# Sixteen experts taken in turns of their groups, with the first results gathered while the last weights are split

## The chip, the cores and the metric

The kernel runs on one core of a Trainium2 chip. Its time is the device time of that core in microseconds (us), the median of several executions; lower is better. The engines that matter here are PE (TensorE, matmuls), DVE (VectorE), ACT (ScalarE) and POOL (GpSimd), which also issues the indirect DMAs (gathers by a list of row numbers), and SP (SyncE), which issues all the other DMAs. Each engine works through its own queue in order.

## The reference

One layer of a decoder trunk over 1024 tokens (and 16 meta tokens) of width 1024: four token mixers, a norm, and then a hierarchical mixture of experts, which alone the change touches. A token picks the best of 4 groups and then the best two of the 4 experts in that group; its output is the weighted sum of the two experts' results, added to the scaled residual stream and normed.

```python
g_sel = jnp.argmax(g_logit, -1)
p_grp = jnp.take_along_axis(jax.nn.softmax(g_logit, -1), g_sel[:, None], 1)
e_logit = jnp.take_along_axis(e_logit, g_sel[:, None, None], 1)[:, 0]     # the 4 experts of that group
top_val, top_idx = lax.top_k(e_logit, TOP_K_INNER)                         # TOP_K_INNER = 2
w = jax.nn.softmax(top_val, -1) * p_grp
e_idx = g_sel[:, None] * EXPERTS_PER_GROUP + top_idx
...
for e in range(N_EXPERTS):                                                 # N_EXPERTS = 16, N_GROUPS = 4
    hid = jax.nn.silu(xf @ w_gate[e]) * (xf @ w_up[e])
    y = y + gate[:, e:e + 1] * (hid @ w_down[e])
...
h = _layer_norm(DN_ALPHA * h + moe_out, ln2_g[l], ln2_b[l])
```

## The kernel before

The mixers and their projections take most of the time; the change does not touch them. Then `Routing.norm` and `Routing.route` norm and route the tokens in 8 tiles of 128. `route` finds the group and the two experts with `max` and `max_index` on DVE and writes them as two one-hot tiles `A[0]` and `A[1]` of 128x16 (tokens by experts); from running counts of these it gives each token a row in the list of each of its two experts. An expert's list holds `CAP` = 192 rows; what goes beyond that is done in a loop after the main part, which runs as often as a count `nov` in memory says, with the expert's number read from `ovx`.

`Experts` runs the 16 experts one after the other. For each one POOL gathers 192 token rows (`xg`, two gathers of 96), PE transposes them (`xT`), and the three weights of the expert come in as six pieces of 128x1024 (512 KB each) on SP's queue. Each piece (`raw`) is split into a rounded part by ACT (`s4h`, `mT0h`, ...) and a rest (`s4l`, ...) by a subtraction, on DVE or POOL: `Pieces.low` asks the planner which of the two would be done sooner. The order of the products is gate of expert e, down of e-1, up of e. `hidden` makes the activations in between: `sg` and `su` are the gate's and up's sums, `th` their product, and `hdh`, `hdl` its two parts, which the down product `py` multiplies. The down result goes through ACT (`ey`) to a DRAM tensor `ys` of 192 rows per expert.

`rest` (written once, in the middle of the expert stage) turns places into `slot`: for each token the rows in `ys` of its two results, the smaller row first, and the weights `wt` in the same order. `ahead` gathers the first result of each of the 8 token tiles from `ys` (`y`, 8 gathers of 512 KB, six buffers, `AHEAD` = 6) and adds it to the residual `h` on DVE. It is started at the place where the last store but one has been written into the program, and reads `ys` up to the 15th expert. `finish` then gathers the second results (`z` and `y`, 8 gathers), which need the last expert's store, adds them, takes mean and variance, norms, and stores the output tile by tile. It uses a square root on ACT, for which `ahead` loads the table with a small activation `t` beforehand.

Everything on PE, DVE, ACT and POOL is put in order by a planner (`Order`): it estimates each engine's time as the program is written, and `Order.run` takes the next step of whichever stream is due at the planner's time of PE. On the chip each engine follows that order, whatever the true times are. The streams of the expert stage, in order of rank, are `hidden`, `tokens`, `rest` and `ahead`; `main`, with PE's products, fills what is left:

```python
o.run([(0, None, x.hidden(W2)), (1, None, x.tokens(W2, ps, scale)), (2, lambda: x.gathered > 2, r.rest(W3, ps, k.ovx, k.ovo, k.nov)),
       (3, lambda: x.stored == NE - 1, ahead(k, x.ys, r))], x.main(W2, ps, free))
```

In the profile nearly all work of the planner has one line, L268 (the helper that records it); tiles tell it apart. `finish` is at L2889 to L2928, its gathers at L2848.

Of the kernel before, what the change touches and what calls it, by code (L numbers as in the profile page):

```python
# [13 lines left out]
OP = mybir.AluOpType  # L14
# [2058 lines left out]
NE = 16  # L2073
CAP = 192
# [96 lines left out]
class Project:  # L2171
# [11 lines left out]
    def more(self):  # L2183

        j = len(self.hs)
        if j < 8:
            self.hs.append(self.pc.add([(self.k.hd[j * 128:j * 128 + 128], lambda r: r)], None))
# [74 lines left out]
class Routing:  # L2262
# [83 lines left out]
    def route(self, j, W, ps):  # L2346

        nc = self.k.nc
        yield from nc.wait(lambda: self.hot == j and j in self.ready)
        lg, mg, me, At = self.lg[:, j], self.mg[:, j], self.me[:, j], self.At[:, j]  # L2350
        A = [a[:, j] for a in self.A]
        ix = W.tile([128, 3, 8], U32, name="mi", bufs=2)
        ng, sel = W.tile([128, 4], F32, name="ng", bufs=2), W.tile([128, 16], F32, name="sel", bufs=2)

        def where(out, i, op):
            n = out.shape[1]
            nc.vector.tensor_tensor(out, self.num[:, 0:n], ix[:, i, 0:1].to_broadcast([128, n]), op=op)

        nc.vector.max(mg, lg[:, 16:24])
        yield  # L2360
        nc.vector.max_index(ix[:, 0], mg, lg[:, 16:24])
        yield
        where(ng, 0, OP.not_equal)
        yield

        nc.vector.scalar_tensor_tensor(sel.rearrange("p (g e) -> p g e", g=4), ng[:, :, None].to_broadcast([128, 4, 4]), -3e38,
# [3 lines left out]
        yield  # L2370
        nc.vector.max_index(ix[:, 1], me[:, 0:8], sel)
        yield
        where(A[0], 1, OP.is_equal)
        yield

        nc.vector.scalar_tensor_tensor(sel, A[0], -3e38, sel, op0=OP.mult, op1=OP.add)
        yield
        nc.vector.max_index(ix[:, 2], me[:, 1:9], sel)
        yield
        where(A[1], 2, OP.is_equal)  # L2380
        yield
        nc.vector.tensor_add(At, A[0], A[1])
        self.hot = j + 1
# [3 lines left out]
        p = ps.tile([128, 512], F32, name="mz", bufs=4)  # L2387
# [5 lines left out]
        s, y = W.tile([128, 2], F32, name="sf"), W.tile([128, 2, 16], F32, name="sy")  # L2393
# [9 lines left out]
        x = self.pix[0:HB, 32 * (j % 2):32 * (j % 2) + 32]  # L2403
# [13 lines left out]
    def rest(self, W, ps, ovx, ovo, nov):  # L2417


        k, nc = self.k, self.k.nc  # L2420
        def t(name, n=1, dt=F32):
            return W.tile([128, 8, n], dt, name=name)
# [17 lines left out]
        p = ps.tile([128, 512], F32, name="py", bufs=4)  # L2440
# [30 lines left out]
        a, b, so, fs = t("oa"), t("ob8"), t("so", 2), t("fs", 2)  # L2471
# [33 lines left out]
        ob, oo, oj = (W.tile([1, 16], F32, name=n) for n in ("ob", "oo", "oj"))  # L2505
# [12 lines left out]
        nc.vector.scalar_tensor_tensor(oj, oo, -float(CAP), oj, op0=OP.mult, op1=OP.add)  # L2518
        nc.vector.scalar_tensor_tensor(oj, ob, float(ROOM), oj, op0=OP.mult, op1=OP.add)
        nc.vector.tensor_scalar(oj, oj, 0.0, float(ROOM * NE - CAP), op0=OP.max, op1=OP.min)  # L2520
        nc.vector.tensor_copy(ovx, ob)
        nc.vector.tensor_copy(ovo, oj)
        nc.vector.tensor_copy(nov, inc[0:1, 15:16])


class Experts:


    def __init__(self, k, I, pieces, h1d, ids, ys, more):
        self.k, self.h1d, self.ids, self.ys, self.pc = k, h1d, ids, ys, pieces  # L2530
        wg, wu, wd = (I["moe_w_" + n][0] for n in ("gate", "up", "down"))
        self.at = {}
        self.order = [("g", 0), ("u", 0)]
        for e in range(1, NE):
            self.order += [("g", e), ("d", e - 1), ("u", e)]
        self.order.append(("d", NE - 1))
        self.used = n = 0
        more()
        for what, e in self.order:
            for m in range(2):  # L2540
                if what == "d":
                    src = (wd[e][m * 128:m * 128 + 128], lambda r: r)
                else:

                    src = ((wg if what == "g" else wu)[e][m * 512:m * 512 + 512].rearrange("(a p) c -> p a c", p=128),
                           lambda r: r.rearrange("p (a c) -> p a c", a=4))
                self.at[what, e, m] = pieces.add([src], lambda n=n: self.place(n), True)
                n += 1
                more()
        self.slots, self.xT, self.acc, self.th, self.hid = [], {}, {}, {}, {}  # L2550
        self.gathered = self.products = self.stored = 0
# [295 lines left out]
def gather(k, ys, ix, y):  # L2847
    k.nc.gpsimd.indirect_dma_start(out=y, out_offset=None, in_=ys, in_offset=bass.IndirectOffsetOnAxis(ap=ix, axis=0))  # L2848


def ahead(k, ys, r):


    nc, pend = k.nc, []

    def add():
        j, y, t = pend.pop(0)
        h = k.h1[j // 4][:, j % 4]
        yield t
        nc.vector.scalar_tensor_tensor(h, y, r.wt[:, j, 0:1], h, op0=OP.mult, op1=OP.add)  # L2860

    for j in range(8):
        if j >= AHEAD:
            yield from add()
        y = k.Y.tile([128, D], F32, name="y", bufs=AHEAD)
        gather(k, ys[0:(NE - 1) * CAP], r.slot[:, j, 0:1], y)
        pend.append((j, y, nc.end))
        yield 0.0
    t = k.Y.tile([128, 1], F32, name="t")
    nc.scalar.activation(t, k.eps, AF.Sqrt)  # L2870
    while pend:
        yield from add()
# [84 lines left out]
def trunk(k, ctx, E, I, pieces, m, x, r):  # L2957
# [45 lines left out]
    W2 = es_x.enter_context(tc.tile_pool(name="xw", bufs=1, **left))  # L3003
    W3 = es_x.enter_context(tc.tile_pool(name="rtr", bufs=1, **left))
    ps = es_x.enter_context(tc.tile_pool(name="xps", bufs=1, space=PSUM))
# [8 lines left out]
    def free():  # L3014
# [3 lines left out]
        for i, n in enumerate(("ln2_g", "ln2_b")):  # L3018
            o.sync.dma_start(k.gb2[:, i], dap(I[n], 0, [[0, 128], [1, D]]))

    o.run([(0, None, x.hidden(W2)), (1, None, x.tokens(W2, ps, scale)), (2, lambda: x.gathered > 2, r.rest(W3, ps, k.ovx, k.ovo, k.nov)),
           (3, lambda: x.stored == NE - 1, ahead(k, x.ys, r))], x.main(W2, ps, free))
    es_x.close()


# [62 lines left out]
```

## Time and profile before

| what | us |
|---|---|
| median of 3 runs (lowest, highest) | 1682.43 (1677.73, 1683.59) |
| the profiled execution | 1686.26 |
| its span | 1684.5 |
| PE busy in the span | 1587.0 (94%) |
| expert products on PE, end of the last `py` | 1631.98 |
| first gather of `finish` begins on POOL | 1640.59 |
| last `fo` product of `finish` begins on PE | 1673.80 |

The profiled execution lies 1.76 us above its span and 3.83 us above the median. The span is read here from its end: the expert stage runs from about 1360 to 1632 us and `finish` from there on; the times in the rows below are counted from the start of the span.

### The profile page before, as it was taken

The page shows a single profiled execution, that of the slowest core. Times are in us where ns is not written, and L with a number is a line of the kernel's source. Part 1 is how long each engine was busy: PE and PEld are TensorE (multiplying, and loading weights), DVE is VectorE, ACT ScalarE, POOL GpSimd, SP SyncE. Part 2 cuts the span into 40 slices and gives each one's busy share as a digit, 9 for nine tenths or more (in the row PEclk, how much of TensorE's full clock was granted, in tenths as well). Part 3 has the DMA queues.
Part 4 walks back from the last instruction along what each step waited for, and adds up shares of the span by engine and source line. Part 5 has one row for each costly group of instructions (what it writes and reads, how often), then busy time and mean ns, then how long its engine had stood idle before and what let it go on. Part 6 is the DMA issues. An engine that isn't in the chain of part 4 may idle for free. (4 is left out here: it accounts for less than half of the span.)

```text
span 1684.5 us, 27808 instructions
## 1 busy us (share of the span) xinstructions
PE 1587.0 (94%) x10020; PEld 1336.2 (79%) x10020; DVE 1114.9 (66%) x2534; ACT 755.7 (45%) x1544; POOL 431.0 (26%) x555
## 2 busy tenths in 40 slices
PE   4999999899999999999999999997999989999985
PEld 3999899788887777777887777775788778898962
DVE  8344755754489898884556477748666668776655
ACT  4334444355544455425444433432121157776645
POOL 5222226831111102123211131126800123111021
PEclk9999999999999999999999998998999989999997
DMA  7874445242322323343211252067512379999855
GB/s 245 240 231 133 146 132 146 80 124 78 91 67 78 83 79 104 95 154 108 69 38 32 86 152 63 28 193 251 180 66 101 126 213 265 287 303 279 269 196 201
DMA packets 240429, 244.86 MB, mean 145 GB/s; under 512 B 39018, under 2 KB 204812, under 8 KB 240288
## 3 DMA queue, kind: packets, MB, share of 16 engines
q1 hardware_dynamic: 234400, 222.08, 43.8%
q0 software_dynamic: 5888, 20.97, 4.4%
q8 instruction: 80, 1.31, 0.3%
q14 instruction: 61, 0.50, 0.1%
HBM read 168.98 MB, written 74.02 MB: 144 GB/s over the span
## 5 line engine op out<-in xcount | busy, mean ns | idle before, releaser
L268 PE MATMUL pj<-hTl,wh 128*128 128x512 f32 (+3 forms) x1184 | 435.5, 368 | 1.0 <-DVE hTl L268 1.0
L268 PE MATMUL pj<-hTh,wh 128*128 128x512 f32 (+3 forms) x1184 | 435.2, 368 | 0.0
L268 PE MATMUL pj<-hTh,wl 128*128 128x512 f32 (+3 forms) x1184 | 431.5, 364 | 0.0
L268 PEld LDWEIGHTS pj<-hTh,wh 128*128 128x128 f32 (+1 forms) x1184 | 225.8, 191 | 26.8 <-issue 2.5
L268 PEld LDWEIGHTS pj<-hTl,wh 128*128 128x128 f32 (+1 forms) x1184 | 225.6, 191 | 26.5 <-issue 1.6
L268 POOL TENSOR_TENSOR wl<-wr,wh 128x256 fp32r<-128x256 f32 (+1 forms) x177 | 137.8, 795 | 422.9 <-ACT wh L268 407.0
L268 PEld LDWEIGHTS pj<-hTh,wl 128*128 128x128 f32 (+1 forms) x1184 | 226.0, 191 | 23.7 <-issue 1.6
L268 ACT COPY pe<-pj 128x384 f32<-128x384 f32 (+3 forms) x84 | 37.4, 445 | 121.9 <-PE pj L268 83.7
L268 DVE SCALAR_TENSOR_TENSOR sc<-rl,wi,sc 128x512 f32<-128x512 f32 (+3 forms) x77 | 58.7, 762 | 42.4 <-ACT rl L268 39.3
L268 ACT CAST wh<-wr 128x256 fp32r<-128x256 f32 (+1 forms) x240 | 85.1, 402 | 1.0 <-DMA wr<-in_w_in_dram 0.9
L268 ACT ACTIVATE pe<-pj 128x512 f32<-128x512 f32 x64 | 38.1, 595 | 100.4 <-PE pj L268 74.8
L268 POOL TENSOR_TENSOR h<-h,g 128x512 f32<-128x512 f32 x46 | 64.7, 1420 | 51.9 <-issue 32.2
L268 POOL DMA_INDIRECT xg<-h1d,ix x32 | 33.7, 1054 | 155.4 <-PE py L268 148.7
L268 ACT ACT_TABLE_LOAD x47 | 60.3, 1283 | 6.3 <-DVE qk L268 2.6
L268 PE MATMUL pg<-xT,mT0h 128*128 128x384 f32 x208 | 62.4, 362 | 0.0
L268 POOL TENSOR_TENSOR sc<-sc,band 128x256 f32<-128x256 f32 (+1 forms) x32 | 24.4, 764 | 124.1 <-DVE sc L268 84.8
L268 PE MATMUL pg<-xT,mT0l 128*128 128x192 f32 x208 | 53.8, 259 | 0.0
L268 DVE TENSOR_TENSOR mT0l<-raw,mT0h 128x1024 fp32r<-128x1024 f32 x35 | 42.5, 1219 | 14.5 <-ACT mT0h L268 13.0
L268 ACT COPY PT<-xb 128x512 f32<-128x512 f32 (+3 forms) x56 | 27.4, 490 | 54.9 <-PE xb L268 52.7
L268 PEld LDWEIGHTS po<-v,PT 128*128 128x128 f32 x352 | 46.3, 192 | 5.6 <-ACT PT L268 2.5
L268 DVE TENSOR_TENSOR wl<-wr,wh 128x256 fp32r<-128x256 f32 x63 | 39.9, 653 | 12.9 <-ACT wh L268 12.8
L268 PE MATMUL po<-v,PT 128*128 128x64 f32 x352 | 47.6, 273 | 0.5 <-ACT PT L268 0.4
(645 smaller groups left out, 3769.5 us busy)
## 6 DMA issues: line engine op xcount, KB each, us to landing
wr<-in_w_in_dram SPq DMA_DIRECT2D x59, 512.0 KB
raw<-in_moe_w_gate_dram SPq DMA_DIRECT2D x32, 512.0 KB
raw<-in_moe_w_up_dram SPq DMA_DIRECT2D x32, 512.0 KB
raw<-in_moe_w_down_dram SPq DMA_DIRECT2D x32, 512.0 KB
gtd<-pe SPq DMA_DIRECT2D x52, 256.0 KB
g<-gtd SPq DMA_DIRECT2D x52, 256.0 KB
ys<-ey SPq DMA_DIRECT2D x14, 768.0 KB
ys<-zero SPq DMA_DIRECT2D x8, 960.0 KB
```

Of the source, the lines that this page charges most:

```text
L268: r = f(*args, **kw)
```

## The change

Three things are changed.

1. The experts are taken in another order. At place e of the order the weights are those of expert `own(e)` = e % 4 * 4 + e // 4, so the first four places are the first experts of the four groups, the next four their second experts, and so on. `route` writes its one-hot tiles in that order (`turns`), with the 16 columns as 4x4 in another stride, and `rest` turns places back into expert numbers for the loop behind (five more DVE instructions on 1x16). The two experts of a token lie in one group and so in two different quarters of the order: the smaller of its two rows belongs to one of the first twelve places.
2. `ahead` therefore reads `ys` up to the twelfth expert alone, and is put into the program where all but the last two weight pieces have been taken for splitting, no longer behind the store of the last expert but one.
3. Ahead of its gathers stands a DVE copy of `slot` onto itself, which the gathers (they read `slot`) must wait for.

```diff
+        def turns(a):
+            return a.rearrange("p (a g) -> p g a", g=4)
+
+        def chosen(out, i):
+            nc.vector.tensor_tensor(turns(out), self.num.rearrange("p (g a) -> p g a", g=4), ix[:, i, 0:1, None].to_broadcast([128, 4, 4]), op=OP.is_equal)
...
-        where(A[0], 1, OP.is_equal)
-        yield
-
-        nc.vector.scalar_tensor_tensor(sel, A[0], -3e38, sel, op0=OP.mult, op1=OP.add)
+        chosen(A[0], 1)
+        yield
+
+        s3 = sel.rearrange("p (g a) -> p g a", g=4)
+        nc.vector.scalar_tensor_tensor(s3, turns(A[0]), -3e38, s3, op0=OP.mult, op1=OP.add)
...
+        nc.vector.tensor_scalar(oo, ob, 4.0, None, op0=OP.is_ge)
+        for i in (8, 12):
+            nc.vector.scalar_tensor_tensor(oo, ob, float(i), oo, op0=OP.is_ge, op1=OP.add)
+        nc.vector.tensor_scalar(ob, ob, 4.0, None, op0=OP.mult)
+        nc.vector.scalar_tensor_tensor(ob, oo, -15.0, ob, op0=OP.mult, op1=OP.add)
...
+def own(e):
+    return e % 4 * 4 + e // 4
...
-                    src = (wd[e][m * 128:m * 128 + 128], lambda r: r)
+                    src = (wd[own(e)][m * 128:m * 128 + 128], lambda r: r)
...
+    nc.vector.tensor_copy(r.slot[:, :, 0:1], r.slot[:, :, 0:1])
     for j in range(8):
         if j >= AHEAD:
             yield from add()
         y = k.Y.tile([128, D], F32, name="y", bufs=AHEAD)
-        gather(k, ys[0:(NE - 1) * CAP], r.slot[:, j, 0:1], y)
+        gather(k, ys[0:(NE - 4) * CAP], r.slot[:, j, 0:1], y)
...
-           (3, lambda: x.stored == NE - 1, ahead(k, x.ys, r))], x.main(W2, ps, free))
+           (3, lambda: hasattr(k, "Y") and pieces.n >= len(pieces.items) - 2, ahead(k, x.ys, r))], x.main(W2, ps, free))
```

The planner puts DVE, ACT and POOL in another order at two places; PE's order is the same instruction for instruction.

At the end of the expert stage, DVE before, from the up sum `su` of the expert at place 14 (places are counted from 0 to 15) to the end of the stage; `h` is the residual and `y` a first result:

```order
L268 TENSOR_TENSOR su<-pg,su 128x192 x2
L268 TENSOR_TENSOR th<-th,su 128x384
L268 TENSOR_TENSOR s9l<-raw,s9h 128x1024
L268 TENSOR_TENSOR hdl<-th,hdh 128x384
L268 TENSOR_TENSOR s4l<-raw,s4h 128x1024
L268 TENSOR_TENSOR sg<-pg,sg 128x192 x2
L268 SCALAR_TENSOR_TENSOR th<-th,sg 128x384
L268 TENSOR_TENSOR s5l<-raw,s5h 128x1024
L268 TENSOR_TENSOR su<-pg,su 128x192 x2
L268 TENSOR_TENSOR th<-th,su 128x384
L268 TENSOR_TENSOR hdl<-th,hdh 128x384
L268 SCALAR_TENSOR_TENSOR h_9910<-y,wt,h_9910 128x1024 x4
```

The same stretch of DVE in the changed kernel, from the copy on:

```order
L268 COPY slot<-slot 128x8
L268 TENSOR_TENSOR th<-th,su 128x384
L268 TENSOR_TENSOR s9l<-raw,s9h 128x1024
L268 TENSOR_TENSOR hdl<-th,hdh 128x384
L268 SCALAR_TENSOR_TENSOR h_9910<-y,wt,h_9910 128x1024
L268 TENSOR_TENSOR s4l<-raw,s4h 128x1024
L268 SCALAR_TENSOR_TENSOR h_9910<-y,wt,h_9910 128x1024
L268 TENSOR_TENSOR sg<-pg,sg 128x192 x2
L268 SCALAR_TENSOR_TENSOR h_9910<-y,wt,h_9910 128x1024 x2
L268 SCALAR_TENSOR_TENSOR h_9911<-y,wt,h_9911 128x1024
L268 SCALAR_TENSOR_TENSOR th<-th,sg 128x384
L268 SCALAR_TENSOR_TENSOR h_9911<-y,wt,h_9911 128x1024 x3
```

The eight additions of first results, which stood behind the last `hdl`, now stand ahead of the last `su`, `th` and `hdl` (these three follow the last row). The last `s5l` has gone to POOL, behind the gathers, and so has an earlier one in the middle of the stage. POOL, before against after:

```order
 L268 IOTA oj 1x16
 L268 TENSOR_TENSOR mT0l_12417<-raw,mT0h_12413 128x1024
+L268 TENSOR_TENSOR s5l<-raw,s5h 128x1024
 L268 DMA xg<-h1d,ix 96x1024 x20
 L268 DMA y<-ys,slot 128x1024 x8
-L2848 DMA z_16532<-ys,slot 128x1024
-L2848 DMA z_16533<-ys,slot 128x1024
-L2848 DMA y<-ys,slot 128x1024 x6
+L268 TENSOR_TENSOR s5l<-raw,s5h 128x1024
```

At the earlier of these two, around the place 4 of the order, DVE had this before (`oj`, `ob`, `ovx` are the small tiles of `rest`):

```order
L268 TENSOR_SCALAR oj<-oj 1x16
L268 CAST ovx<-ob 1x16
L268 CAST ovo<-oj 1x16
L268 CAST nov<-inc 1x1
L268 TENSOR_TENSOR th<-th,su 128x384
L268 TENSOR_TENSOR xT<-py,xT 128x4x96 x2
L268 TENSOR_TENSOR s5l<-raw,s5h 128x1024
L268 TENSOR_TENSOR hdl<-th,hdh 128x384
L268 TENSOR_TENSOR s6l<-raw,s6h 128x1024
L268 TENSOR_TENSOR xT<-py,xT 128x4x96
```

and has this now:

```order
L268 TENSOR_SCALAR oj<-oj 1x16
L268 TENSOR_SCALAR oo<-ob 1x16
L268 SCALAR_TENSOR_TENSOR oo<-ob,oo 1x16 x2
L268 TENSOR_SCALAR ob<-ob 1x16
L268 SCALAR_TENSOR_TENSOR ob<-oo,ob 1x16
L268 CAST ovx<-ob 1x16
L268 CAST ovo<-oj 1x16
L268 CAST nov<-inc 1x1
L268 TENSOR_TENSOR th<-th,su 128x384
L268 TENSOR_TENSOR xT<-py,xT 128x4x96 x3
L268 TENSOR_TENSOR s6l<-raw,s6h 128x1024
L268 TENSOR_TENSOR hdl<-th,hdh 128x384
```

Five small instructions stand ahead of `th`, and `hdl`, which the down product waits for, has moved behind the third `xT` and `s6l`. On ACT the small square root `t` has moved ahead of the last gate's tanh:

```order
L268 CAST s4h<-raw 128x1024
L268 ACT_TABLE_LOAD
L268 ACTIVATE t<-eps_94 128x1
L268 COPY sg<-pg 128x192 x2
L268 COPY ey<-py 96x512
L268 CAST s5h<-raw 128x1024
L268 ACT_TABLE_LOAD
L268 ACTIVATE th<-sg 128x384
L268 COPY ey<-py 96x512 x3
```

There the tables are loaded for the square root and then for tanh again, and `finish` (its first square root, `v`) has a third load, which it did not have before.

## Rows read from the trace of the kernel before

**Rows 1.** Windows: busy us of each engine, granted clock, DMA share, GB/s.

```profile
1420.00:1425.00 5.00, 4.06 (x18) 2.88 (x19) 4.03 (x8) 4.19 (x9) 0.00 (x0) 1.00 1.05 266
...
1500.00:1550.00 50.00, 50.00 (x325) 44.81 (x325) 35.24 (x53) 35.51 (x64) 6.93 (x7) 1.00 1.02 293
...
1625.00:1630.00 5.00, 5.00 (x16) 3.31 (x16) 2.34 (x3) 1.60 (x3) 4.09 (x4) 0.66 0.96 342
...
1639.00:1640.00 1.00, 0.00 (x0) 0.00 (x0) 1.00 (x2) 0.00 (x0) 0.00 (x0) 1.00 0.39 160
```

**Rows 2.** Timeline of PE: start, us, what, [idle before it, what ended that].

```profile
1420.94 0.47 PE L268 MATMUL py<-s8h,hdl 128*96 128x512 f32 x1 [1.23 <-DVE hdl L268]
...
1624.46 0.48 PE L268 MATMUL py<-s4h,hdh 128*96 128x512 f32 x1 [1.99 <-ACT hdh L268]
```

**Rows 3.** Timeline of DVE in the middle of the expert stage.

```profile
1393.48 2.47 DVE L268 TENSOR_TENSOR ov<-sl,A 128x128 f32<-128x128 f32 x1 [0.35 <-POOL sl L268]
...
1396.30 0.29 DVE L268 TENSOR_TENSOR ov<-sl,A 128x128 f32<-128x128 f32 x1
...
1414.05 2.02 DVE L268 TENSOR_SCALAR ob<-ob 1x16 f32<-1x16 f32 x1
...
1417.44 0.19 DVE L268 TENSOR_SCALAR oj<-oj 1x16 f32<-1x16 f32 x1
...
1417.82 0.54 DVE L268 TENSOR_TENSOR th<-th,su 128x384 f32<-128x384 f32 x1
1418.29 1.00 DVE L268 TENSOR_TENSOR xT<-py,xT 128x384 fp32r<-128x384 f32 x2
1419.22 1.20 DVE L268 TENSOR_TENSOR s5l<-raw,s5h 128x1024 fp32r<-128x1024 f32 x1
1420.35 0.54 DVE L268 TENSOR_TENSOR hdl<-th,hdh 128x384 fp32r<-128x384 f32 x1
```

**Rows 4.** Timeline of POOL in the same stretch.

```profile
1393.41 2.39 POOL L268 TENSOR_TENSOR s7l<-raw,s7h 128x1024 fp32r<-128x1024 f32 x1
...
1410.97 5.08 POOL L268 TENSOR_TENSOR mT0l<-raw,mT0h 128x1024 fp32r<-128x1024 f32 x1 [9.81 <-ACT mT0h L268]
1416.19 0.93 POOL L268 DMA_INDIRECT xg<-h1d,ix  x1
```

**Rows 5.** Timeline of ACT in the same stretch.

```profile
1415.94 1.05 ACT L268 CAST s5h<-raw 128x1024 fp32r<-128x1024 f32 x1 [0.80 <-DMA raw<-in_moe_w_down_dram]
```

**Rows 6.** Timeline of DVE at the end of the expert stage.

```profile
1608.33 0.62 DVE L268 TENSOR_TENSOR su<-pg,su 128x192 f32<-128x192 f32 x2
...
1622.58 0.64 DVE L268 TENSOR_TENSOR su<-pg,su 128x192 f32<-128x192 f32 x2 [5.25 <-ACT su L268]
...
1626.72 1.28 DVE L268 SCALAR_TENSOR_TENSOR h<-y,wt,h 128x1024 f32<-128x1024 f32 x1 [1.72 <-DMA y<-ys,slot]
...
1638.44 3.77 DVE L268 SCALAR_TENSOR_TENSOR h<-y,wt,h 128x1024 f32<-128x1024 f32 x3 [3.46 <-DMA y<-ys,slot]
```

**Rows 7.** Timeline of POOL there: first of eight `y` gathers, first of `finish`.

```profile
1622.46 0.96 POOL L268 DMA_INDIRECT y<-ys,slot  x1 [56.94 <-PE pg L268]
...
1640.59 1.20 POOL L2848 DMA_INDIRECT z<-ys,slot  x1 [6.45 <-DMA ys<-ey]
```

**Rows 8.** The chain that ended last, there: start, us, what.

```profile
1612.40 5.55 PE py L268 x24
...
1624.46 7.51 PE py L268 x24
...
1632.61 7.19 DMA ys<-ey
```

**Rows 9.** Timeline of ACT there and at the start of `finish`.

```profile
1629.57 1.28 ACT L268 ACT_TABLE_LOAD   x1
1630.86 0.20 ACT L268 ACTIVATE t<-eps 128x1 f32<-128x1 f32 x1
...
1649.02 0.20 ACT L2923 ACTIVATE m<-s 128x1 f32<-128x1 f32 x1 [0.57 <-DVE h L2922]
```

More of the change, by code (lines that the diff above doesn't have):

```diff
@@ L2353, in route @@
         ng, sel = W.tile([128, 4], F32, name="ng", bufs=2), W.tile([128, 16], F32, name="sel", bufs=2)
-        def where(out, i, op):
-            n = out.shape[1]
-            nc.vector.tensor_tensor(out, self.num[:, 0:n], ix[:, i, 0:1].to_broadcast([128, n]), op=op)
+        def turns(a):
+            return a.rearrange("p (a g) -> p g a", g=4)
+        def chosen(out, i):
+            nc.vector.tensor_tensor(turns(out), self.num.rearrange("p (g a) -> p g a", g=4), ix[:, i, 0:1, None].to_broadcast([128, 4, 4]), op=OP.is_equal)
         nc.vector.max(mg, lg[:, 16:24])
@@ L2362, in route @@
         yield
-        where(ng, 0, OP.not_equal)
+        nc.vector.tensor_tensor(ng, self.num[:, 0:4], ix[:, 0, 0:1].to_broadcast([128, 4]), op=OP.not_equal)
         yield
@@ L2379, in route @@
         yield
-        where(A[1], 2, OP.is_equal)
+        chosen(A[1], 2)
         yield
@@ L2541, in __init__ @@
                 if what == "d":
-                    src = (wd[e][m * 128:m * 128 + 128], lambda r: r)
+                    src = (wd[own(e)][m * 128:m * 128 + 128], lambda r: r)
                 else:
-                    src = ((wg if what == "g" else wu)[e][m * 512:m * 512 + 512].rearrange("(a p) c -> p a c", p=128),
+                    src = ((wg if what == "g" else wu)[own(e)][m * 512:m * 512 + 512].rearrange("(a p) c -> p a c", p=128),
                            lambda r: r.rearrange("p (a c) -> p a c", a=4))
```

## The prediction

> **What bounds the kernel now.** I read the chain of waits first: from the first expert products to the last, nearly every piece of it is PE. The windows show it as well: in the middle of the stage PE is busy for all of 50.00 us [rows 1], and its timeline gives no wait between the one of 1.23 us at 1420.94 and the one of 1.99 us at 1624.46 [rows 2]. Between these two nothing but PE's own work counts, and a delay of PE at 1421 arrives at the end in full. Behind 1622 the bound is a relay: PE's last products wait for DVE's `su`, `th`, `hdl`, the last store takes 7.19 us [rows 8], `finish` waits for it with its first gather until 1640.59 [rows 7], and from there ACT and DVE alternate. So there are two things to cost: what the change does to DVE at the few places where PE waits for it, and what it does to the last store and to `finish`.
>
> **What it may give back.** The store takes 7.19 us [rows 8] because the eight gathers of first results run at the same time: the DMA share is 0.96 in 1625 to 1630 and falls to 0.39 in 1639 to 1640 [rows 1]. From the end of the last products (1624.46 + 7.51 = 1631.97) to the first gather of `finish` are 8.62 us. The store of place 14 shows the same way without that traffic: its products end at 1612.40 + 5.55 = 1617.95 [rows 8] and the gather that it releases starts at 1622.46 [rows 7], 4.51 us. If the gathers are over by then, 4.1 us are won there. That is all there is to win.
>
> **The end of the stage.** The copy of `slot` stands behind `su` of place 14, which ends at 1608.33 + 0.62 = 1608.95 [rows 6]; with 0.1 us for the copy (an estimate from the 0.19 us that a small one takes [rows 3]; nothing to 0.2 us either way) the gathers are free at 1609.05. POOL began its first gather of `finish` 0.79 us after the store had landed (1632.61 + 7.19 = 1639.80 [rows 8] to 1640.59 [rows 7]), so it starts at 1609.84, 12.6 us sooner than before. The first result was there 4.26 us after such a start (1622.46 [rows 7] to 1626.72 [rows 6]): now at 1614.1. All eight gathers and the two stores beside them kept the DMAs going until about 1639.4 (0.39 of the second from 1639 [rows 1]), 16.9 us after the start. Now the two stores of place 14 fall into the same stretch, so the last result is there at about 1626.8 and its addition (1.28 us [rows 6]) ends at 1628.1.
>
> The price is where the additions stand. DVE takes all eight of them ahead of the last `su`, and each waits for its gather. `su` began at 1622.58 [rows 6]; now it begins at 1628.1. From `su` to PE's products were 1.88 us (1622.58 to 1624.46 [rows 2]), so these begin at 1630.0, 5.5 us later, with PE waiting. They take 7.51 us as before, part of it at the lower clock, and 4.51 us later `finish` starts its gather, at 1642.0: **1.4 us later** than 1640.59. The gain of 4.1 us is more than spent. The low end: the stores of place 14, 0.79 of 4.98 MB, pass without holding up a gather; they are 16% of the transfer, 2.4 us, and the result is -1.0. The high end: the additions end as late after the start as before (1638.44 + 3.77 = 1642.21 [rows 6], 19.75 us after it), at 1629.6; then it is 2.9. I take 1.4, since bytes are what these DMAs are short of. Queued behind the waiting additions are also `s4l` and the gate's `sg` and `th`; nobody needs them before the last products, so they cost nothing as long as the last `su` is later still. The last `s5l` on POOL stands behind the eight gathers, done about 1620 plus at most 5.08 us (the longest such subtraction [rows 4]): covered by the same wait of PE.
>
> ACT has two more table loads there, at 1612 and 1616, which delay the copies `ey` of place 14 by under 3 us; DVE's waiting covers that too. The third, in `finish`, is on the path: the load takes 1.28 us [rows 9] between the first square and the first square root, and ACT then had 0.57 us of idle time ahead of the next `m` [rows 9]. That leaves **0.7 us** (0.7 to 1.3, the latter if the second result comes sooner). The rows show no more to it than these 1.28 us: the next ACTIVATE starts at 1630.86, straight behind the load [rows 9]. The Trainium skill (ScalarE: Activation LUTs, What ACT_TABLE_LOAD costs) gives a drain of about 1.38 us on top of a load of 1.28. By that the term would be about 2.1 instead of 0.7; the trace agrees with the load and shows no drain.
>
> **The middle of the stage.** PE waits for `hdl` at 1420.94 [rows 2]. Ahead of that `hdl` the change puts five small DVE instructions at 0.19 us [rows 3], 0.95 us, and it moves `hdl` behind one more `xT` (0.47 us, half of the 0.93 from 1418.29 to 1419.22 [rows 3]) and behind `s6l`, which takes the place of an equal `s5l`. That is 1.4 us. `s5l` itself has gone to POOL, ready when ACT is done at 1415.94 + 1.05 = 1416.99 [rows 5], and such a subtraction on POOL stops DVE: while POOL did one in 2.39 us at 1393.41 [rows 4], DVE's `ov`, begun 0.07 us later, took 2.47 us where the same shape took 0.29 [rows 3], and the one at 1410.97 [rows 4] ends together with a DVE instruction on 16 numbers that took 2.02 [rows 3]. So up to 2.2 us more, 3.6 in all; some of it may lie beside the `xT`, which read PSUM and which no row shows together with POOL. I take **3.0** between 1.4 and 3.6, nearer to the upper end since it happened in both of these rows. The Trainium skill (SBUF — State Buffer, SBUF: two separate sides) says that DVE and GpSimd take a common port by an exclusive lock, and that the loser blocks for the whole instruction. The trace agrees (2.47 against 0.29 us); by that rule the term would be 3.6, not 3.0.
>
> PE's wait there grows from 1.23 to some 4 us. Behind the 1.23 us the granted clock stayed at 1.00 [rows 1]; behind the 1.99 us at 1624.46 it was 0.66 in the window from 1625 [rows 1], and 24 products took 7.51 us instead of 5.55 [rows 8]. The new wait is nearer to the latter, so I add **2.0 us** for a stretch at half clock (0 at the low end).
>
> **Taken as free.** The one-hot tiles in 4x4 strides are 16 DVE instructions on 16 numbers of some 0.2 us each, two on the path of the last token tile: 0 taken, up to 0.4. The weights come from other addresses in equal pieces; PE never waits for a weight while the DMA share is 1.02 [rows 1], so there is little to lose: 0. The token gathers behind the new `s5l` on POOL (at 1416.19 [rows 4]) start up to 5 us later; their rows are transposed an expert later, and that hides it; uncovered they would cost up to 5.
>
> **The sum.** 3.0 + 2.0 + 1.4 + 0.7 = 7.1 us. The profiled execution of 1686.26 us (span 1684.5) would become 1693.4; it lies 3.83 above the median of the runs, 1682.43, which I move by the same amount: **1689.5 us**. About 0.5% (8.4 us: below 1674.0, above 1690.8) is what a measurement of this kernel can tell from no change.
>
> **The rivals.** *The middle costs little*: POOL's subtraction lies beside the `xT` and the clock stays up. 1.4 + 1.4 + 0.7 = 3.5, 1685.9. For it speaks that no row shows `xT` held up. *The order does what it is for*: the gathers land at POOL's pace of issue, 1.25 us apart; the last is there at 1609.84 + 4.26 + 7 x 1.25 = 1622.9, its addition ends at 1624.1, PE resumes at 1626.0, and `finish` starts at 1638.0, 2.6 us sooner; with 0.7 and 1.4 that is -0.5, 1681.9. Against it speaks a DMA share of 0.96 with the same transfers. Even with no wait at all it could not exceed 4.1 - 0.7 = 3.4 us, far from 0.5%. *Slower*: the gathers land late. Place: the last three additions ahead of the last `su`; before, the sixth waited 3.46 us for its gather [rows 6], behind the stores. If they end 19.75 us after the start again, `finish` is 1.5 us later: 8.6 us, 1691.0. It decides from 1629.4 on for the end of the last addition; and if the products behind the long wait ran wholly at half clock (11.1 us instead of 7.51), 3.6 more. *The change doesn't do what it says*: POOL's first gather still waits for something as late as before, until 1622.46. Then the additions end at 1642.2, PE resumes at 1644.1, `finish` starts at 1656.1, and the sum is 15.5 + 0.7 + 5.0 = 21.2, 1703.6. Against it speaks that the gathers read only the first twelve places, whose stores are long done.
>
> **How the numbers follow.** Forecast 0.40, the cheap middle 0.22, the aim reached 0.05, late gathers 0.29, no early start 0.04. Low sum: 1.4 + 0 - 1.0 + 0.7 = 1.1, 1683.5; high sum: 3.6 + 2.0 + 2.9 + 1.3 = 9.8, 1692.2, and a little for the spread of the runs: 1683 to 1693, which leaves out the aim reached, the missing start and a few of the late ones. Faster by over 0.5%: 0.03, only by a scatter of the runs. Slower by over 0.5%: the late gathers, the missing start and 0.02 of the forecast, 0.35. Within: 0.62.
>
> **What would show it.** In the profile of the changed kernel: the first `y` gather on POOL some 13 us before the last up products end; DVE's additions each with idle time put down to the DMA of `y`; PE waiting about 7 us ahead of the last `py`; the last `ys` store landing in 3 to 4 us; the first `z` gather 1 to 3 us later, counted from PE's last up product; a table load ahead of the first `v`. In the middle: PE's wait for `hdl` at 3 to 5 us, a DVE instruction of over 2 us beside POOL's `s5l`, and a granted clock below 1.00 right behind. The forecast is wrong if the last addition ends before the last up sum is due, or if PE's wait in the middle stays under 2 us.

## The result and the profile after

The changed kernel takes 1688.08 us (median; 1681.61 to 1696.48), the kernel before 1678.39 us beside it (1672.99 to 1683.64): ratio 1.0052, 95% interval 1.0038 to 1.0066, or 9.7 us more. The profiled execution took 1687.11 us with a span of 1685.4, against 1686.26 and 1684.5 before.

Spans hide most of this. The mixers ahead of the expert stage vary from execution to execution: POOL's `mT0l`, with which the middle begins, starts at 1410.97 us in the trace of before [rows 4], at 1401.86 in that of after, and anywhere from 1398 to 1411 in the traces below. So the stage is read here by distances between four marks on POOL: the start of `mT0l`, the next token gather that is more than 20 us behind it, the last token gather, and the first `z` gather of `finish`. POOL of the changed kernel, timeline (start, us, what, [idle before it, what ended that]):

```profile
1401.86 5.08 POOL L268 TENSOR_TENSOR mT0l<-raw,mT0h 128x1024 fp32r<-128x1024 f32 x1 [9.80 <-ACT mT0h L268]
1407.93 2.39 POOL L268 TENSOR_TENSOR s5l<-raw,s5h 128x1024 fp32r<-128x1024 f32 x1 [0.99 <-ACT s5h L268]
...
1428.71 0.98 POOL L268 DMA_INDIRECT xg<-h1d,ix  x1 [15.53 <-PE py L268]
...
1561.00 0.91 POOL L268 DMA_INDIRECT xg<-h1d,ix  x1 [1.82 <-DMA raw<-in_moe_w_up_dram]
1606.67 1.49 POOL L268 DMA_INDIRECT y<-ys,slot  x1 [44.76 <-DVE th L268]
...
1618.25 2.58 POOL L268 TENSOR_TENSOR s5l<-raw,s5h 128x1024 fp32r<-128x1024 f32 x1
1641.01 0.94 POOL L2863 DMA_INDIRECT z<-ys,slot  x1 [20.18 <-issue]
```

The second and third mark in the kernel before (`mT0l` is in [rows 4], `z` in [rows 7]):

```profile
1432.80 0.98 POOL L268 DMA_INDIRECT xg<-h1d,ix  x1 [14.44 <-PE py L268]
...
1564.37 1.15 POOL L268 DMA_INDIRECT xg<-h1d,ix  x1 [1.44 <-PE py L268]
```

The middle takes 26.85 us instead of 21.83 (+5.02), the long stretch behind it 132.29 instead of 131.57 (+0.72), the end of the stage 80.01 instead of 76.22 (+3.79), and `finish` to the end of the span 44.39 instead of 43.91 (+0.48). These add up to 10.0 us; the medians differ by 9.7, and the ratio makes it 8.7. PE's two waits, and the first and last of the 24 products of the last expert:

```profile
1413.05 0.74 PE L268 MATMUL py<-s8h,hdh 128*96 128x512 f32 x1 [3.29 <-ACT hdh L268]
...
1415.45 0.74 PE L268 MATMUL py<-s8h,hdl 128*96 128x512 f32 x1 [1.23 <-DVE hdl L268]
...
1628.21 0.74 PE L268 MATMUL py<-s4h,hdh 128*96 128x512 f32 x1 [9.08 <-ACT hdh L268]
...
1636.06 0.40 PE L268 MATMUL py<-s5h,hdl 128*96 128x512 f32 x1
```

The first two answer the single 1.23 us of [rows 2]; the third answers its 1.99. The first of the 24 products has 0.74 us here and 0.48 there. The windows around both waits (columns as in [rows 1]; the clock is the number ahead of the DMA share) show the granted clock at 0.67, 0.65, 0.50 and 0.64; 0.50 is the lower of its two levels, 1.2 of 2.4 GHz, and the other windows hold a part of each:

```profile
1410.00:1415.00 5.00, 1.17 (x2) 0.39 (x2) 4.76 (x17) 1.90 (x4) 2.74 (x3) 0.67 0.83 227
1415.00:1420.00 5.00, 4.55 (x14) 3.08 (x15) 2.42 (x5) 2.61 (x4) 0.00 (x0) 0.65 0.74 249
1625.00:1630.00 5.00, 1.79 (x4) 1.18 (x5) 2.94 (x5) 0.51 (x1) 0.00 (x0) 0.50 0.00 0
1630.00:1635.00 5.00, 5.00 (x16) 3.35 (x15) 0.00 (x0) 1.17 (x2) 0.00 (x0) 0.64 0.00 0
```

DVE in the middle, where PE waits for the down products of place 2 while the tokens of place 4 are transposed:

```profile
1407.96 2.39 DVE L268 SCALAR_TENSOR_TENSOR oj<-oo,oj 1x16 f32<-1x16 f32 x1
...
1410.66 0.15 DVE L268 TENSOR_SCALAR oo<-ob 1x16 f32<-1x16 f32 x1
...
1411.63 0.16 DVE L268 CAST ovx<-ob 1x16 int32<-1x16 f32 x1
...
1412.32 1.47 DVE L268 TENSOR_TENSOR xT<-py,xT 128x384 fp32r<-128x384 f32 x3
1413.72 1.20 DVE L268 TENSOR_TENSOR s6l<-raw,s6h 128x1024 fp32r<-128x1024 f32 x1
1414.85 0.54 DVE L268 TENSOR_TENSOR hdl<-th,hdh 128x384 fp32r<-128x384 f32 x1
```

An instruction on 16 numbers, 0.15 us in the kernel before, takes 2.39 us, begun 0.03 us behind POOL's `s5l` of 2.39 us. The five small instructions take 0.97 us (1410.66 to 1411.63).

DVE at the end, from the copy of `slot` to the last `su`:

```profile
1605.52 0.16 DVE L268 COPY slot<-slot 128x8 int32<-128x8 int32 x1
...
1612.04 1.28 DVE L268 SCALAR_TENSOR_TENSOR h<-y,wt,h 128x1024 f32<-128x1024 f32 x1 [4.25 <-DMA y<-ys,slot]
...
1616.15 5.76 DVE L268 SCALAR_TENSOR_TENSOR h<-y,wt,h 128x1024 f32<-128x1024 f32 x3
...
1625.15 1.28 DVE L268 SCALAR_TENSOR_TENSOR h<-y,wt,h 128x1024 f32<-128x1024 f32 x1 [0.38 <-DMA y<-ys,slot]
1626.35 0.62 DVE L268 TENSOR_TENSOR su<-pg,su 128x192 f32<-128x192 f32 x2
```

Three additions take 5.76 us beside POOL's second `s5l` (1618.25 above), and the last one, which waits 0.38 us for its gather, ends at 1626.43, 19.76 us behind the start of the first gather. In `finish` ACT has the third table load:

```profile
1648.13 1.28 ACT L2943 ACT_TABLE_LOAD   x1
1649.43 0.29 ACT L2943 ACTIVATE v<-v,eps 128x1 f32<-128x1 f32 x1
```

### The profile page after: what moved, and what is told of

Read it like the earlier page. It is cut to its first block, busy times and chain, and to the rows that moved or that the text cites. A ratio compares the mean times of both kernels' runs of the same rounds, so it can differ in the third digit from the quotient of the medians.

```text
span 1685.4 us, 27813 instructions
## 1 busy us (share of the span) xinstructions
PE 1576.3 (94%) x10020; PEld 1327.2 (79%) x10020; DVE 1118.2 (66%) x2538; ACT 758.8 (45%) x1546; POOL 432.8 (26%) x557
```

## The experiments

All kernels are built from the changed one. "Time" is the median, with that of the kernel before measured beside it; the four stretches are those of the traces between the marks above, in us. "py" is the length of the last 24 products.

| kernel | time (before) | ratio, 95% interval | middle | long | end | finish | py |
|---|---|---|---|---|---|---|---|
| before | | | 21.83 | 131.57 | 76.22 | 43.91 | 7.51 |
| changed | 1688.08 (1678.39) | 1.0052, 1.0038–1.0066 | 26.85 | 132.29 | 80.01 | 44.39 | 8.25 |
| A order of experts alone | 1685.45 (1679.73) | 1.0020, 1.0001–1.0039 | 27.41 | 131.26 | 75.10 | 44.01 | 7.36 |
| B the same without the five | 1679.08 (1679.73) | 0.9992, 0.9969–1.0016 | 21.83 | 131.77 | 76.75 | 43.69 | 7.44 |
| C whole without the five | 1683.90 (1679.73) | 1.0019, 0.9999–1.0039 | 21.84 | 131.26 | 80.06 | 44.32 | 8.50 |
| D C with additions behind `hdl` | 1677.30 (1679.73) | 0.9981, 0.9959–1.0003 | 21.84 | 131.26 | 72.90 | 43.96 | 7.50 |
| E both `s5l` on DVE | 1688.04 (1679.27) | 1.0051, 1.0034–1.0068 | 27.41 | 131.26 | 78.54 | 44.30 | 7.91 |
| F useless products in the waits | 1684.72 (1679.27) | 1.0037, 1.0017–1.0057 | 25.01 | 131.26 | 78.14 | 43.86 | 5.92 |
| G complete, rearranged | 1674.08 (1679.27) | 0.9963, 0.9944–0.9983 | 21.82 | 132.64 | 72.11 | 44.23 | 7.42 |
| H G with useless products | 1678.24 (1679.27) | 0.9985, 0.9964–1.0006 | 21.83 | 131.26 | 71.79 | 43.58 | 5.92 |
| I no `s5l` on POOL in the middle | 1688.29 (1679.15) | 1.0057, 1.0038–1.0075 | 25.93 | 131.26 | 79.45 | 43.93 | 7.47 |
| J table loaded late | 1689.70 (1679.15) | 1.0063, 1.0043–1.0083 | 26.85 | 131.26 | 80.58 | 43.29 | 8.56 |
| K G once more | 1675.20 (1679.15) | 0.9984, 0.9962–1.0006 | 21.84 | 131.46 | 70.63 | 43.82 | 5.94 |

An interval reaches some 3 us to either side, and a ratio need not be that of the two medians (A lies 5.7 us above the kernel before by the medians, 3.4 by the ratio). So sizes are read from the traces, and the times bear out the larger ones. Each trace is one execution: before, A and B, which have the same order at the end, show 75.10 to 76.75 us there.

The long stretch and `finish` hold no difference of more than some tenths that follows the kernels: the +0.72 us of the changed kernel in the long stretch (one more wait of PE, 0.76 us) is in none of C, E, F, I and J, and G and K, the same program, differ there by 1.2.

### A and B: the order of experts, with and without the five small instructions

A takes the third part of the change and the early start out again:

```diff
-    nc.vector.tensor_copy(r.slot[:, :, 0:1], r.slot[:, :, 0:1])
...
-        gather(k, ys[0:(NE - 4) * CAP], r.slot[:, j, 0:1], y)
+        gather(k, ys[0:(NE - 1) * CAP], r.slot[:, j, 0:1], y)
...
-           (3, lambda: hasattr(k, "Y") and pieces.n >= len(pieces.items) - 2, ahead(k, x.ys, r))], x.main(W2, ps, free))
+           (3, lambda: x.stored == NE - 1, ahead(k, x.ys, r))], x.main(W2, ps, free))
```

> The experts in turns alone: the first results are gathered as in the kernel before, behind the store of the last expert but one. DVE, ACT and POOL differ from before only in the middle of the expert stage (five small DVE instructions, one subtraction on POOL, hdl later) and in the strides of the one-hot tiles. My theory: the middle costs 5 us (3 of waiting, 2 of half clock), so 5 us over the kernel before, PE's waits ahead of hdl at 4 to 5 us in all, and a last store of about 7 us as before. Rival (the early additions are the whole of the loss): 0 to 1 us. Rival (other experts in other places are slower all along): about 5 to 9 us, but spread over the stage.

B takes the five instructions out as well (C and D leave them out too), so that places stand in `ovx` for expert numbers:

```diff
-        nc.vector.tensor_scalar(oo, ob, 4.0, None, op0=OP.is_ge)
-        for i in (8, 12):
-            nc.vector.scalar_tensor_tensor(oo, ob, float(i), oo, op0=OP.is_ge, op1=OP.add)
-        nc.vector.tensor_scalar(ob, ob, 4.0, None, op0=OP.mult)
-        nc.vector.scalar_tensor_tensor(ob, oo, -15.0, ob, op0=OP.mult, op1=OP.add)
```

> As the one before, but without the five small instructions that turn places into expert numbers for the loop behind the main part (left out; the loop does not run on this data). Then the planner puts DVE, ACT and POOL in the same order as in the kernel before. My theory: 0 us against the kernel before (-1 to 1). Rival (other weights' addresses, other lists or the strided one-hot tiles cost time): as much as the experts in turns with those five.

A's middle is 5.58 us longer and nothing else in it is; its time is 5.7 us above the kernel before. B's middle is that of the kernel before to 0.01 us, its time the same within the interval. So the order of the experts, its addresses and its strided one-hot tiles cost nothing that shows (B's interval reaches up to 2.7 us), and what the middle costs comes in whole with five instructions of 0.15 us: they take 0.97 us themselves, and the planner, which counts them, moves `s5l` to POOL and `hdl` back.

### C and D: the early gathers, with the additions ahead of and behind the last `hdl`

C is the whole change without the five instructions. D lets `ahead` wait with its additions until the last `hdl` is written; its table load moves behind the last tanh with them, and `s5l` comes back to DVE:

```diff
     for j in range(8):
+        if j == AHEAD:
+            yield from nc.wait(lambda: NE - 1 in x.made)
         if j >= AHEAD:
             yield from add()
```

> The whole change without the five small instructions (left out as above): the middle is as in the kernel before, the early gathers and additions are as in the change. My theory: the end of the stage alone costs 4 to 5 us (additions ahead of the last su 7 us, down products at half clock 0.8, a table load 0.7, less 4.1 from the store). Rival (the middle is the whole of the loss): 0 or a gain of up to 3.

> As the one before, but the additions of the first results stand behind the last hdl; the first six gathers start as early as in the change. The square root's table is loaded behind the last tanh again, and the last s5l is back on DVE. My theory: only the gain is left, the last store lands in 3 to 4 us instead of 7, PE's last wait is 2 us: 4 us faster than the kernel before. Rival (the early transfers themselves disturb the last weights or the products): no gain, or slower. Rival (gathers seven and eight, which need a buffer that an addition frees, collide with the store): a gain of 1 to 2 us.

C's end is 3.84 us longer than before, its time 4.2 us above; with A's 5.7 that makes 9.9, the whole by the medians. By the ratios it is 6.6 of 8.7, and by the traces A's middle and C's end make 9.4 of 10.0. D's end is 3.3 us shorter than before: the store is won and PE's last wait is 1.99 us again. Its time is 2.4 us below the kernel before, short of the 4 expected, and the interval still touches 1. POOL of D says where the rest is:

```profile
1608.78 0.94 POOL L268 DMA_INDIRECT y<-ys,slot  x1 [0.30 <-issue]
1617.56 1.73 POOL L268 DMA_INDIRECT y<-ys,slot  x1 [7.85 <-DVE h L268]
1619.60 0.94 POOL L268 DMA_INDIRECT y<-ys,slot  x1 [0.30 <-issue]
1628.34 0.94 POOL L2860 DMA_INDIRECT z<-ys,slot  x1 [7.80 <-issue]
```

With six buffers the seventh and eighth gather wait for the first additions (7.85 us) and so run beside the last store; 5.28 us pass from the end of the products to `z`, against 4.55 in the changed kernel.

### E and I: does POOL's subtraction hold DVE up?

E forbids POOL for the two pieces whose `s5l` it had taken, I for all pieces in the middle behind `mT0l` (there the second `s5l`, at the end, stays on POOL); `n` is the number of the piece:

```diff
-            (nc.gpsimd if self.aside else nc.sooner(1024) if pool_lo else nc.vector).tensor_sub(lo, raw, hi.bitcast(F32))
+            (nc.gpsimd if self.aside else nc.sooner(1024) if pool_lo and n not in (41, 111) else nc.vector).tensor_sub(lo, raw, hi.bitcast(F32))
...
+            (nc.gpsimd if self.aside else nc.sooner(1024) if pool_lo and not 41 <= n < 50 else nc.vector).tensor_sub(lo, raw, hi.bitcast(F32))
```

> The whole change, with the two subtractions s5l that had gone to POOL put back on DVE; everything else is written as in the changed kernel. In the middle DVE has the last hdl behind the five small instructions, three xT and one subtraction, as in the changed kernel, but no POOL subtraction runs beside them (the planner then puts a later one, s6l, on POOL behind two token gathers). Theory, that POOL's subtraction holds DVE up: the 2.39 us of DVE's instruction on 16 numbers shrink to about 0.2, PE's wait ahead of these down products falls from 3.29 + 1.23 us to about 1.2 + 1.4, and the middle costs 1.4 to 3.4 us instead of 5.0; about 3 us less than the changed kernel in all. Rival, that the five small instructions and hdl's later place cost the 5 us by themselves: the wait stays above 4 us and the time is that of the changed kernel. At the end of the stage the addition of 3.37 us becomes one of 1.28, and nothing is won by that, since the last gather lands no sooner.

In the middle E told nothing apart: the planner put the next subtraction, `s6l`, on POOL two gathers later, and it met another small instruction. POOL and DVE of E:

```profile
1412.60 2.35 POOL L268 TENSOR_TENSOR s6l<-raw,s6h 128x1024 fp32r<-128x1024 f32 x1
```

```profile
1412.70 2.27 DVE L268 CAST ovx<-ob 1x16 int32<-1x16 f32 x1
...
1619.21 3.66 DVE L268 SCALAR_TENSOR_TENSOR h<-y,wt,h 128x1024 f32<-128x1024 f32 x3
...
1624.40 3.66 DVE L268 SCALAR_TENSOR_TENSOR h<-y,wt,h 128x1024 f32<-128x1024 f32 x3
```

The long instruction has moved with POOL's subtraction from `oj` to `ovx`, and E is 8.8 us above the kernel before, where 3 us below the changed kernel were expected. At the end of the stage, where E was expected to win nothing, the last addition ends 18.63 us behind the first gather instead of 19.76, and the end is 78.54 us instead of 80.01, which the times don't show. POOL's `s5l` is only a part of that. The last of the eight gathers on POOL, in the changed kernel and in E, and the last three additions of C on DVE:

```profile
1616.93 1.31 POOL L268 DMA_INDIRECT y<-ys,slot  x1 [0.30 <-issue]
```

```profile
1619.02 0.94 POOL L268 DMA_INDIRECT y<-ys,slot  x1 [0.59 <-DVE sg L268]
```

```profile
1620.88 3.67 DVE L268 SCALAR_TENSOR_TENSOR h<-y,wt,h 128x1024 f32<-128x1024 f32 x3
```

In the changed kernel this gather lands 8.2 us behind its start, 18.46 us behind the first one's, and the last addition waits for it; had POOL not held the additions before, DVE would only have waited longer. F, I and J are alike: their last addition waits 1.04, 0.55 and 0.53 us for its gather. In E the gather lands 6.8 us behind its start, 16.4 us behind the first one's, and the additions run without a wait. C has the same early landing (16.4) with `s5l` on POOL, and its last addition ends after 19.57 us. So `s5l` on POOL costs 0.9 us more than on DVE where the gather lands early (C against E), and nothing in the traces whose last gather lands late. Why it lands early in C and E is open. It isn't that `s5l`: C has it on POOL, and G, H and K, which do not, have the last gather there after 17.9 to 18.9 us.

> The changed kernel with no subtraction on POOL in the middle of the stage after mT0l: s5l and the ones behind it are on DVE. DVE then has ahead of that hdl the five small instructions (0.97 us), one more xT (0.47) and one more subtraction (1.13) than the kernel before, 2.57 us. Counted from the start of POOL's mT0l, hdl began at 9.97 us plus 0.59 before PE took it in the kernel before, and PE's product with hdl stood at 9.97 (before), 13.59 (changed kernel), 13.53 (with s6l on POOL in the place of s5l). Theory, that the long instruction on 16 numbers (2.39, 2.27 us) is long because POOL subtracts at the same time: no such instruction is left behind mT0l's end, the product with hdl stands at about 12.5, the middle costs 2.6 us and up to 2.0 for half clock, against 5.0. Rival, that such a long instruction comes by itself (DVE waits for something else there): it stays, the product stands at 14 or later, the middle costs 5 us or more. In all 0.5 to 2.5 us below the changed kernel by the theory.

```profile
1415.13 0.16 DVE L268 CAST ovx<-ob 1x16 int32<-1x16 f32 x1
...
1418.35 1.20 DVE L268 TENSOR_TENSOR s6l<-raw,s6h 128x1024 fp32r<-128x1024 f32 x1
1419.49 0.54 DVE L268 TENSOR_TENSOR hdl<-th,hdh 128x384 fp32r<-128x384 f32 x1
```

In I, with no subtraction on POOL there, every small instruction behind the end of `mT0l` takes 0.13 to 0.19 us (`ovx`, for one). PE's product with `hdl` stands 12.55 us behind the start of `mT0l`, as the theory had it (12.5), where it is 9.97 before and 13.59 in the changed kernel. The theory holds. The time doesn't fall with it (9.1 us above before): I swaps a hold of 2.24 us for a subtraction of 1.13 on DVE, which leaves 0.9 us of gain in the middle, below what the times tell.

### F: are the products slow because PE stood idle?

```diff
+WARM = {2: 28, 15: 76}
...
+                        for _ in range(WARM.get(e, 0) if b + u == 0 else 0):
+                            nc.nc.tensor.matmul(p[:, 256:512], self.ones[:, 0:128], self.ones, start=True, stop=True)
```

> The whole change, with matrix products of no use (128x256 on a constant tile, about 0.115 us each) put on PE into its two long waits: 28 ahead of the down products in the middle, 76 ahead of the last down products. Nothing else moves. Theory, that PE's standing idle is what puts the products behind it at half clock: the last products take about 5.6 us instead of 8.26, finish's first gather starts 2.7 us sooner, the middle costs about 3 instead of 5.0 us; together about -4.7 us against the changed kernel. Rival, that the clock there falls for another reason: 8.26 us stay, and the time is that of the changed kernel or up to 0.5 more.

PE of F at both places, and the windows behind them:

```profile
1416.53 3.23 PE L2692 MATMUL py<-ones 128*128 128x256 bf16 x28
1419.51 0.48 PE L268 MATMUL py<-s8h,hdh 128*96 128x512 f32 x1
...
1622.97 8.47 PE L2692 MATMUL py<-ones 128*128 128x256 bf16 x76
1632.65 0.47 PE L268 MATMUL py<-s4h,hdh 128*96 128x512 f32 x1 [1.20 <-ACT hdh L268]
```

```profile
1420.00:1425.00 5.00, 3.33 (x15) 2.22 (x15) 3.28 (x7) 3.26 (x7) 0.00 (x0) 1.00 0.91 271
1630.00:1635.00 5.00, 3.80 (x24) 2.57 (x22) 2.52 (x5) 1.07 (x2) 0.00 (x0) 1.00 0.00 0
```

The granted clock stays at 1.00, the last products take 5.92 us instead of 8.25, and `hdl`'s lateness alone is left in the middle (25.01, +3.18). By the traces F's middle is 1.84 us shorter than that of the changed kernel and its end 1.87, 3.7 of the 4.7 expected. By the medians F lies 5.5 us above the kernel before and the changed kernel 9.7, but these intervals overlap. With PE kept busy the products behind both waits are not slow, in this one trace; without that, the products behind waits of 8 to 9 us are slow in all five others at the end. So it is PE's standing idle, not something else in these places, that the lower clock follows.

### J: the third table load

```diff
+    while pend:
+        yield from add()
     t = k.Y.tile([128, 1], F32, name="t")
     nc.scalar.activation(t, k.eps, AF.Sqrt)
-    while pend:
-        yield from add()
```

> The changed kernel with the small square root t behind the last addition of a first result, so that its table is loaded after the last tanh; nothing else moves but that three additions close up. Theory, that the third table load is on the path of finish with 0.7 us: no load ahead of finish's first v, and from finish's first gather to the end 43.9 us as before instead of 44.4; 0.3 to 0.7 us less than the changed kernel, which the times cannot tell, only the trace. Rival: the load had been covered, no difference.

`finish` takes 43.29 us without the load against 44.39, but the scatter is as large as the effect: the five traces with the load (changed, C, E, F, I) have 43.86 to 44.39, mean 44.16, the eight without it 43.29 to 44.23, mean 43.81. That is 0.35 us, not settled closer than by some tenths.

### G, H and K: the same idea, put together

G keeps all that the change computes. The five instructions move to the end of `ahead`, where DVE has nothing to do, and only the first two additions stay ahead of the last `su`, so that all eight gathers can start early:

```diff
+    yield from nc.wait(lambda: NE - 1 in x.made)
     t = k.Y.tile([128, 1], F32, name="t")
     nc.scalar.activation(t, k.eps, AF.Sqrt)
     while pend:
         yield from add()
+    ob, oo = r.ob, r.oo
+    nc.vector.tensor_scalar(oo, ob, 4.0, None, op0=OP.is_ge)
...
+    nc.vector.tensor_copy(k.ovx, ob)
```

> A complete kernel with the early gathers: the five small instructions stand at the very end of the expert stage on DVE, the additions of the third to the eighth first result and the square root t stand behind the last hdl, and only the first two additions, whose gathers land first, stand ahead of the last su. Both s5l are on DVE. Theory, that the order of experts with early gathers is worth the 4.1 us of the last store once nothing stands in the way of hdl: PE's wait ahead of the last down products is 1.99 us as before, the store lands 3 to 4 us after its issue, finish's first gather starts about 12 us after the last products' start instead of 16.1, the time is 4 us below the kernel before. Rival, that the seventh and eighth gather still run beside the store: -2.4 us, as with all additions behind hdl.

> The kernel with the moved additions and small instructions, with 16 products of no use on PE in the wait of 1.99 us ahead of the last down products. Theory of the clock: these take about 5.6 us instead of 7.5, 1.9 us less than without, about 6 us below the kernel before. Rival: no difference to the kernel without them.

> The complete kernel with moved additions and small instructions once more, for its time: in its first trace the stretch from the last token gather to finish's first gather was 4.1 us shorter than in the kernel before. Theory: 4 us below the kernel before, ratio 0.9975. Rival: a part of the 5 us by which its runs lay lower was scatter of the mixers' part, and the ratio comes out at 0.999 or above.

PE, DVE and POOL of G, one row each:

```profile
1621.69 0.47 PE L268 MATMUL py<-s4h,hdh 128*96 128x512 f32 x1 [1.99 <-ACT hdh L268]
```

```profile
1622.14 7.26 DVE L268 SCALAR_TENSOR_TENSOR h<-y,wt,h 128x1024 f32<-128x1024 f32 x6
```

```profile
1633.67 0.94 POOL L2860 DMA_INDIRECT z<-ys,slot  x1 [15.23 <-issue]
```

PE waits 1.99 us as before, six additions lie beside its last products, and `z` starts 11.98 us behind the start of these products instead of 16.13: the end is 4.11 us shorter than before, as expected. The times say the same in two measurements, 5.2 us (interval below 1) and 4.0 us below the kernel before (ratio 0.9984, interval just over 1). H has G's program with 16 useless products ahead of the last ones (`WARM = {15: 16}`): the clock stays at 1.00 and the products take 5.92 us, but 5.74 us pass from their end to `z` instead of 4.56, so the end is only 0.3 us shorter than G's, and its time is not better; why the store took longer there is open. K, the same program as G, had 5.94 us of products without any useless ones and 4.56 us behind them, so H doesn't show that the useless products did anything.

K's products, first and last:

```profile
1611.68 0.47 PE L268 MATMUL py<-s4h,hdh 128*96 128x512 f32 x1 [1.99 <-ACT hdh L268]
...
1617.22 0.40 PE L268 MATMUL py<-s5h,hdl 128*96 128x512 f32 x1
```

## Why the prediction was right, and where its size was off

The forecast was 1689.5 us, the measured time 1688.08. That they lie so close is in part luck: the sum was +7.1 and was added to 1682.43, while the medians beside each other say +9.7 over a kernel before of 1678.39. The late gathers, the rival with +8.6, describe the end of the stage better than the forecast does. Of the signs two failed: two of DVE's eight additions wait for a DMA, not each, and `finish`'s first gather is 3.8 us later where 1 to 3 were said. Step by step:

- **The middle: 3.0 + 2.0 predicted, 5.02 measured.** PE's product with `hdl` comes 3.62 us later (13.59 instead of 9.97 behind the start of `mT0l`): five instructions 0.97, one `xT` 0.47, POOL's hold 2.39 - 0.15 = 2.24, together 3.68. The hold came in full, so this term was at the upper end, 3.6, where 3.0 was taken. The Trainium skill (SBUF — State Buffer, SBUF: two separate sides) says that whoever loses the common lock blocks for the whole of the other's instruction; 2.39 us beside 2.39 here, and 2.27 beside 2.35 in E, agree. The clock cost the other 1.40 (1.9 to 2.0 in A and E), and F, which holds it up, leaves 3.18.
- **The store: 4.1 won, predicted; 4.07 measured.** From the end of the last products (1636.06 + 0.40) to `z` 4.55 us pass, where it was 8.62. A and B, which also gather late, have 7.61 and 9.19, so by the trace that one compares with the gain is 3.1 to 4.6.
- **The start of the gathers: as predicted.** The first one starts 45.67 us behind the last token gather, which would be 1610.04 in the time of the kernel before; 1609.84 was said.
- **The landing of the last gather: the step that was off.** The sum let the last result arrive 16.9 us behind the start of the first gather, the time at which the DMA share of the kernel before had fallen to 0.39, and so the last addition end after 18.3 (1628.1 - 1609.84). But an addition waits for the landing of its gather, and that came later in the kernel before as well:

```profile
1632.63 1.51 POOL L268 DMA_INDIRECT y<-ys,slot  x1 [0.30 <-issue]
```

  This is its last gather of first results. It lands 8.3 us behind its start, at 1640.9, which is 18.5 us behind the start of the first; the last of the three additions in [rows 6] begins there (1642.21 - 1.28 = 1640.93). The 19.75 us of the rival "gathers land late" are this landing and one addition, and the changed kernel repeats them: 18.46 and 19.76. Counted in the time of the kernel before, the last addition ended at 1629.8, behind the 1629.4 from which the prediction gives the case to that rival. The additions did not wait one by one for their gathers: only the first (4.25 us) and the last (0.38) did. POOL's last `s5l`, written off as "covered by the same wait of PE", held three of them up by 2.1 us, which no sum had, but the last one still had to wait, so in this trace it cost nothing. The end of the additions gives 1.5 us; with 0.2 us of the gathers' start, and 0.1 less from there on, PE's last products begin 7.12 us later instead of 5.5.
- **Their length: 7.51 taken, 8.25 measured.** The prediction had priced a longer stretch at half clock as a part of a rival only, though the middle had its 2.0 us for the same cause. The end is thus 7.12 + 0.74 - 4.07 = 3.79 instead of 1.4.
- **The third table load: 0.7 predicted, some 0.35 to 0.5.** The drain that the Trainium skill gives (ScalarE: Activation LUTs, What ACT_TABLE_LOAD costs), by which it would have been about 2.1, is in no trace: in the changed kernel the load is followed by the next ACTIVATE after 0.02 us, and no longer gap stands ahead of it.
- **Taken as free:** strides and addresses cost nothing (B), nor did the token gathers behind POOL's new `s5l`.
- **The low end of the range:** the stores' 16% of 16.9 us are 2.7 and not 2.4, which would put it 0.3 us lower; nothing else rests on it.

So the signs, the hold in the middle and the store held, and the term that was too small is the end of the stage, 3.8 instead of 1.4: 1.5 of it by the landing of the last gather, 0.7 by the products behind the wait. G bears out from the other side what the store is worth: with everything out of its way the end is 4.11 us shorter, and K's 5.59 hold 1.5 of the clock besides.

## What to carry to other kernels

Starting a transfer earlier is worth what it frees at its end (here the last store, about 4 us); the consumers of the transfer must not stand ahead of the critical chain in an in-order queue. Leave them behind it, but for the few whose buffers the next transfers need. A handful of tiny instructions in a planned kernel costs more than its own time, since the planner may answer by moving large ones: put them where the engine is idle, and read the order of every engine, not the diff. When a step creates a wait of the matrix engine, price the clock behind it too. And take the time at which a transfer frees its reader from the reader's row, not from the window in which the DMA share falls.

## What was not expected of the hardware

- An instruction of DVE on 16 numbers can take as long as the POOL subtraction that it meets: 2.39 us beside 2.39, 2.27 beside 2.35, and 0.13 to 0.19 us with no subtraction on POOL (I). Which one is hit is a matter of when POOL begins. But POOL's length alone doesn't tell: beside its `mT0l` of 5.08 us [rows 4] DVE's `s4l` of 128x1024 took its usual 1.20, and only the last instruction beside it was long (2.02 [rows 3]).
- After the same wait of 1.99 us the same program's last products took 7.42 us in one trace and 5.94 in another (G and K). The clock fell behind that wait in one execution and not in the other. Behind the 8 to 9 us of waiting in the changed kernel, C, E, I and J they took 7.47 to 8.56.
